# One load for the first pair's K, the third pair's norms on VectorE and its squares on GpSimd, and all instruction orders written anew

## The chip, the cores and the metric

The kernel runs on one core of a Trainium2 chip. A core has five engines that run side by side, each through its own list of instructions in order: TensorE (PE: matrix products and transposes; its weight loads are listed as PEld), VectorE (DVE), ScalarE (ACT), GpSimd (POOL) and SyncE (SP), which only issues transfers here. They meet through semaphores alone: an instruction waits until those it needs have counted up. TensorE writes to PSUM, a small memory of eight banks; everything else lies in SBUF, and 16 DMA engines carry data between it and the device's memory.

The metric is the device time of one execution in microseconds (us). Lower is better.

## The reference

Attention over cosine similarities: 8 batches of 12 heads, 512 rows of 64 numbers each in Q, K and V, in float32.

```python
Q_norm = Q / (np.linalg.norm(Q, axis=-1, keepdims=True) + 1e-10)
K_norm = K / (np.linalg.norm(K, axis=-1, keepdims=True) + 1e-10)
scores = np.einsum('bhqd,bhkd->bhqk', Q_norm, K_norm) / tau        # tau = 0.1
weights = np.exp(scores - np.max(scores, axis=-1, keepdims=True))
weights = weights / (np.sum(weights, axis=-1, keepdims=True) + 1e-10)
return np.einsum('bhqk,bhkd->bhqd', weights, V).astype(np.float32)
```

The scores lie between -10 and 10, so the kernel takes no maximum off before the exponential. The sum of the weights comes out of the second product, since V carries a column of ones.

## The kernel before, in words

The 96 heads are worked through as 48 pairs of heads, pair 0 to pair 47 (the first pair is pair 0, the third is pair 2). Each step of a pair is one entry with a name; the number behind it is the pair.

- LD.s.0 and LD.s.1 load Q and K of pair s (256 KB each, both heads, line 410), LV.s loads V (line 413). 18 buffers hold Q and K, six hold V.
- SQ.s.0 squares Q and K of a pair in one GpSimd instruction of 128x1024 (line 263). For pairs 1 and 2 Q and K are squared apart: SQ.s.0 (Q) on ScalarE (line 261), SQ.s.1 (K) on GpSimd.
- SSQ.s adds the squares of each row in groups with 16 products on TensorE (line 279), and RED.s.0 on VectorE finishes the sum (line 286). For eight pairs, named DIRECT, VectorE alone does it (line 268, RED.s.0 and RED.s.1).
- The reciprocal square root of the sums is made in one of two ways. For pairs 0 to LOGGED - 1 it is a logarithm and an exponential on ScalarE: LN (line 291) and EX (line 295). For the others it is made on VectorE with a bit trick and two Newton steps: NEW.g.0 to NEW.g.7 (lines 381, 372, 373, 377) for a group g of pairs at once. The group sizes stand in GROUPS, whose last number holds for all the rest.
- SCL.s.0 and SCL.s.1 scale Q and K to bf16 (line 302), Q on VectorE, K on VectorE or GpSimd as the table ON says.
- TR.s transposes both on TensorE (line 309), EVA.s copies the result to SBUF on VectorE (line 462). SSQ and TR use one PSUM bank in turn: who comes next in TensorE's list waits until VectorE has read what was there. For seven pairs K's transposes are a transposing DMA, XT.s (line 453).
- SCO.g are the products of K and Q (line 472) and EXP.g the exponentials on ScalarE (lines 497 and 500). From pair 1 on one EXP takes two blocks of 512 scores, so a pair has four of them. Four PSUM banks hold scores, so an SCO waits for the EXP two before it.
- VC.s copies V to bf16 on GpSimd (line 506), PV.s.h.t are the products of weights and V on TensorE (line 520), RCP.s and NRM.s divide by the sum on VectorE (lines 541 and 543), ST.s stores (line 547). Weights are kept for six pairs, so PV runs some pairs behind EXP.

Pair 0 is treated apart, in the function head(), for the sake of an early start: each half (one head) of Q and K goes its own way. Names carry w (0 for Q, 1 for K) and h (the head): LD.0.w.h (line 324; Q from SyncE's queue, K from ScalarE's), SQ.0.w.h, RED.0.w.h, LN.0.w.h, EX.0.w.h, SCL.0.w.h, TR.0.w.h (line 348), EVA.0.w.h (line 319). K of pair 0 is only copied to bf16 (line 320); its norm goes into the scale of the exponentials EXP.0 to EXP.7, each 128x512. Dummy products, warm.k and fill.k (line 248), stand between TensorE's first steps.

Nothing is scheduled while the kernel runs. A list for each engine, the table ORDER, says in which order its entries are issued, and each entry waits for what it needs. So an entry that waits holds up all entries behind it on its engine.

## Time and profile before

| what | us |
|---|---|
| median of three runs | 194.03 (193.59 to 194.36) |
| the profiled execution | 193.27 |
| its span, from the first to the last instruction | 191.5 |
| ScalarE busy in the span | 183.2 (96%) |
| TensorE busy in the span | 179.0 (93%) |
| GpSimd busy in the span | 154.6 (81%) |
| VectorE busy in the span | 152.0 (79%) |
| start of the first exponential, EXP.0 | 7.94 |
| start of the first exponential of pair 1, EXP.8 | 13.78 |

How to read the lines: in the timeline a row has the start in us, the time it took, the engine, the line of the kernel, the operation, what it writes and reads with the shapes, and how many instructions were merged (xN). In square brackets stand the idle time of the engine just ahead and who ended it. In the groups of instructions the numbers behind the bar are the busy time in us and the mean in ns, behind the second bar the idle time ahead of them. Instructions of one engine overlap: the next can start before the last has ended. In the list of issues, the last number is the time from a transfer's issue to its landing.

### The profile page before, as it was taken

Reading aid. Unit: us, or ns where it says so; the run is one execution under the profiler, and the core shown is the slowest. Engines: PE = TensorE matmul, PEld = TensorE weight load, DVE = VectorE, ACT = ScalarE, POOL = GpSimd, SP = SyncE. Lnnn points to the kernel's source line nnn. Section 1 sums busy time; section 2 is a strip of 40 time slices with the busy share of each in tenths; the row PEclk is TensorE's granted clock in tenths of the full one; section 3 lists DMA queues with packets and bytes.
Section 4 is the critical chain, followed back from the end, with each engine's and each line's share of the span. In section 5 each row is a group of like instructions: output and inputs, shape, how many; then the busy total and the mean of one; then the engine's idle time right before and its main releaser. Section 6 shows DMA issues by size and latency. Waiting matters only on the chain.

```text
span 191.5 us, 7081 instructions
## 1 busy us (share of the span) xinstructions
PE 179.0 (93%) x2940; PEld 116.4 (61%) x2940; DVE 152.0 (79%) x454; ACT 183.2 (96%) x217; POOL 154.6 (81%) x143
## 2 busy tenths in 40 slices
...
GB/s 157 340 354 351 348 350 349 350 240 363 365 363 348 267 356 380 377 233 342 322 330 357 264 361 363 365 304 165 234 323 223 82 58 186 125 55 55 113 78 201
DMA packets 56257, 51.72 MB, mean 270 GB/s; under 512 B 6944, under 2 KB 56224, under 8 KB 56224
## 3 DMA queue, kind: packets, MB, share of 16 engines
...
q10 hardware_dynamic: 432, 0.33, 0.5%
q14 instruction: 10, 0.08, 0.1%
HBM read 37.75 MB, written 12.58 MB: 263 GB/s over the span
## 4 chain that ended last, share of the span: by engine, by line
ACT 50%; PE 32%; POOL 9%; DVE 4%; issue 2%; DMA 2%; SPq 0%; POOLq 0%
ACT et L500 50%; PE scps L472 11%; PE ops L520 11%; POOL sq L263 6%; PE xps L309 4%; PE xps L279 3%; DMA qk<-in_Q_dram 2%; POOL qn L302 1%; POOL vb L506 1%; DVE qt L462 1%; DVE qn L302 1%; PE nps L248 1%; DVE ob L576 1%; PE xps L348 0%; PE nps L559 0%
## 5 line engine op out<-in xcount | busy, mean ns | idle before, releaser
L500 ACT ACTIVATE et<-scps 128x1024 bf16<-128x1024 f32 (+1 forms) x190 | 173.4, 1076 | 0.9 <-PE scps L472 0.8
L263 POOL TENSOR_TENSOR sq<-qk 128x1024 bf16<-128x1024 f32 (+2 forms) x49 | 88.2, 1814 | 2.1 <-DMA qk<-in_K_dram 2.1
L472 PE MATMUL scps<-qt 64*128 64x512 bf16 x384 | 75.7, 386 | 5.3 <-ACT et L500 4.0
L520 PEld LDWEIGHTS ops<-vb,et 128*128 128x128 bf16 x1504 | 53.4, 98 | 25.9 <-issue 15.6
L520 PE MATMUL ops<-vb,et 128*128 128x65 bf16 x1504 | 68.3, 194 | 0.3 <-DVE ob L543 0.2
L302 POOL TENSOR_TENSOR qn<-qk,rk 128x512 bf16<-128x512 f32 x36 | 37.3, 1051 | 13.7 <-DVE rk L377 11.2
L302 DVE TENSOR_TENSOR qn<-qk,nps 128x512 bf16<-128x512 f32 x54 | 35.7, 678 | 0.2
L462 DVE COPY qt<-xps 128x1024 bf16<-128x1024 bf16 (+1 forms) x47 | 30.4, 646 | 6.3 <-PE xps L309 6.0
L543 DVE TENSOR_TENSOR ob<-ops,rd 128x512 f32<-128x512 f32 x47 | 32.4, 690 | 1.0
L472 PEld LDWEIGHTS scps<-qt 64*128 64x128 bf16 x384 | 18.9, 92 | 22.1 <-ACT et L500 7.6
L506 POOL TENSOR_SCALAR vb<-vf 128x512 bf16<-128x512 f32 x48 | 29.6, 635 | 1.7 <-DMA vf<-in_V_dram 1.7
L309 PE MATMUL xps<-ident,qn 128*128 128x128 bf16 x348 | 27.4, 220 | 0.8 <-POOL qn L302 0.7
L279 PEld LDWEIGHTS xps<-sq,ident 128*128 128x128 bf16 x624 | 20.7, 97 | 8.6 <-issue 3.7
L279 PE MATMUL xps<-sq,ident 128*128 128x64 bf16 x624 | 25.0, 192 | 0.9 <-POOL sq L263 0.6
L309 PEld LDWEIGHTS xps<-ident,qn 128*128 128x128 bf16 x348 | 19.7, 98 | 9.3 <-DVE rd L541 2.5
L541 DVE RECIPROCAL rd<-ops 128x8 f32<-128x8 f32 x47 | 9.6, 204 | 11.8 <-PE ops L520 11.4
L286 DVE TENSOR_REDUCE nps<-xps 128x16 f32<-128x64 f32 x37 | 8.5, 230 | 7.1 <-PE xps L279 6.8
L268 DVE TENSOR_REDUCE nps<-sq 128x8 f32<-128x512 bf16 x16 | 10.8, 683 | 0.1
L373 DVE SCALAR_TENSOR_TENSOR nps<-nps,ys 128x32 f32<-128x32 f32 (+1 forms) x46 | 9.0, 196 | 1.1
L372 DVE TENSOR_TENSOR nps<-nps,ys 128x32 f32<-128x32 f32 (+1 forms) x46 | 8.9, 194 | 1.0
L497 ACT ACTIVATE et<-scps,xr 128x512 bf16<-128x512 f32 x8 | 5.1, 684 | 0.0
L377 DVE SCALAR_TENSOR_TENSOR nps<-nps,ys 128x16 f32<-128x16 f32 (+1 forms) x28 | 4.7, 175 | 0.3
...
## 6 DMA issues: line engine op xcount, KB each, us to landing
vf<-in_V_dram SPq DMA_DIRECT2D x48, 256.0 KB, 6.1
qk<-in_K_dram SPq DMA_DIRECT2D x47, 256.0 KB, 6.3
qk<-in_Q_dram SPq DMA_DIRECT2D x47, 256.0 KB, 6.2
out_dram<-ob SPq DMA_DIRECT2D x47, 256.0 KB, 5.0
qk<-in_Q_dram SPq DMA_DIRECT2D x2, 128.0 KB, 2.9
qk<-in_K_dram ACTq DMA_DIRECT2D x2, 128.0 KB, 3.1
out_dram<-ob SPq DMA_DIRECT2D x1, 128.0 KB, 2.1
qt<-qn SPq DMA_TRANSPOSE x7, 4.5
```

The lines of the kernel that those rows point to most:

```text
L263: emit = lambda e: e.tensor_tensor(out=b, in0=a, in1=a, op=ALU.mult)
L268: lambda e: e.tensor_reduce(out=dst, in_=sq[s % R_SQ][:, lo:hi, :], axis=AX.X, op=ALU.add))
L279: last = e.matmul(out=x_ps[:, 0:64], lhsT=ident[:, :], rhs=sq[s % R_SQ][:, :, 4 * k : 4 * k + 4], start=(k == 0), stop=(k == 15))
L302: lambda e: e.tensor_tensor(out=qn[iqn][:, w].rearrange("p t h d -> p h t d"), in0=qk[iq][:, w].rearrange("p h (t d) -> p h t d", t=NT), i ...
L309: last = e.transpose(dst[:, i, :], qn[s % R_QN][:, b // NT, b % NT].rearrange("p h d -> p (h d)"), ident[:, :])
L462: lambda e, lo=lo, hi=hi: e.tensor_copy(out=qt_all[:, lo:hi], in_=tb[:, lo:hi]))
L472: last = e.matmul(out=sc_ps[:, (v + i) % BANKS, :], lhsT=qt[p % R_QT][64 * h : 64 * h + 64, 1, c, :], rhs=qt[p % R_QT][64 * h : 64 * h + 6 ...
L500: P.add(("EXP", g2), "act", needs, lambda e, o=o, i=i: e.activation(out=o, in_=i, func=ACT.Exp, scale=inv_tau))
L506: lambda e: e.tensor_scalar(out=vb[:, iq, :, :, 0:DIM].rearrange("p c h d -> p h c d"), in0=vf[iv][:, :, :].rearrange("p h (c d) -> p h c ...
L520: last = e.matmul(out=bank[:, 65 * t : 65 * t + 65], lhsT=e_block(s, c, h, t), rhs=vb[:, iq, c, h, :], start=(c == 0), stop=(c == NT - 1))
L541: lambda e: e.reciprocal(out=rd[io][:, :], in_=grid[:, :, :, DIM]))
L543: lambda e: e.tensor_tensor(out=ob[io][:, :], in0=grid[:, :, :, 0:DIM], in1=rd[io][:, :].unsqueeze(3).to_broadcast([128, 2, NT, DIM]), op= ...
```

## The change

- Pair 0's K is loaded by one transfer of 256 KB, LD.0.1, for both heads, instead of two of 128 KB. Everything that reads K of pair 0 (SQ.0.1.h, SCL.0.1.h) waits for the whole.
- LOGGED goes from 3 to 2 and GROUPS from [1, 2] to [1, 1, 2]: pair 2's norms are made by Newton steps, as a group of its own. LN.2, EX.2.0 and EX.2.1 disappear from ScalarE's list; there are 24 groups of Newton steps, where there were 23.
- ON gets the entry SQ.2.0, which puts the squares of pair 2's Q on GpSimd.
- FILL goes from 17 to 11: six dummy products fewer.
- All five lists of ORDER are new. K of a pair is now mostly loaded ahead of Q, the first loads go more in the order of the pairs (some K loads, of pairs 5, 6, 9 and 12 among them, stand a few places ahead), and on ScalarE LN.0.0.0 and EX.0.0.0 stand ahead of SQ.0.0.1, and LN.0.1.1 and EX.0.1.1 behind EXP.1.

```diff
     def head():
-        for w, h in ((0, 0), (1, 0), (0, 1), (1, 1)):
-            P.add(("LD", 0, w, h), "act" if w else "sp", ["table"] if w else [], lambda e, w=w, h=h: e.dma_start(
-                out=qk[0][:, w, h], in_=src(K if w else Q, 0)[:, h]), slot=f"first{w}{h}")
+        for h in range(2):
+            P.add(("LD", 0, 0, h), "sp", [], lambda e, h=h: e.dma_start(
+                out=qk[0][:, 0, h], in_=src(Q, 0)[:, h]), slot=f"first{h}")
+        P.add(("LD", 0, 1), "act", ["table"], lambda e: e.dma_start(out=qk[0][:, 1], in_=src(K, 0)), slot="first2")
...
             for w in range(2):
-                squares(0, engine("pool", "SQ", 0, w, h), (w, h), 512 * w + 256 * h, 512 * w + 256 * h + 256, [("LD", 0, w, h)])
+                load = ("LD", 0, 1) if w else ("LD", 0, 0, h)
+                squares(0, engine("pool", "SQ", 0, w, h), (w, h), 512 * w + 256 * h, 512 * w + 256 * h + 256, [load])
...
-GROUPS = [1, 2]
-LOGGED = 3
+GROUPS = [1, 1, 2]
+LOGGED = 2
...
-FILL = 17
-ON = {'SQ.0.0.0': 'act', 'SQ.0.1.0': 'pool', ... 'SCL.17.1': 'dve'}
+FILL = 11
+ON = {'SQ.0.0.0': 'act', 'SQ.0.1.0': 'pool', ... 'SCL.17.1': 'dve', 'SQ.2.0': 'pool'}
 ORDER = {
     "sp": """
-        LD.0.0.0 LD.0.0.1 LD.1.1 LD.1.0 LD.2.0 LD.2.1 LD.3.1 LD.3.0 LD.5.0 LD.4.0 LD.5.1 LV.1 LD.4.1 LV.0 LD.7.0
-        LD.6.1 LD.6.0 LV.2 LD.7.1 LD.8.1 LD.9.1 LD.8.0 LD.9.0 LD.13.1 LD.11.0 LD.11.1 LD.13.0 LV.3 LD.14.0
-        LD.10.1 LD.10.0 LV.4 LV.5 LD.12.1 LV.7 LD.14.1 LV.8 LD.12.0 LD.15.1 LV.9 LD.16.1 LD.19.0 LV.6 LD.15.0
+        LD.0.0.0 LD.0.0.1 LD.1.1 LD.1.0 LD.2.1 LD.2.0 LD.5.1 LD.3.1 LD.3.0 LD.4.1 LD.4.0 LD.6.1 LD.5.0 LD.9.1
+        LD.7.0 LD.6.0 LV.0 LD.7.1 LV.1 LD.8.1 LV.3 LD.8.0 LV.2 LD.12.1 LD.9.0 LD.11.0 LD.13.0 LD.10.1 LD.12.0
+        LV.6 LD.11.1 LD.10.0 LV.4 LD.13.1 LV.5 LD.17.0 LD.17.1 LD.20.1 LD.15.1 LD.19.0 LD.16.0 LV.7 LD.15.0
...
     "pool": """
-        one eye SCL.0.1.0 SQ.0.1.0 SQ.0.1.1 SCL.0.1.1 SQ.1.1 vone SQ.2.1 SCL.1.1 SQ.3.0 SQ.5.0 SQ.4.0 VC.0
-        SQ.6.0 SQ.7.0 VC.2 VC.1 SQ.8.0 SQ.9.0 VC.3 SQ.13.0 SQ.10.0 SQ.11.0 SQ.14.0 VC.5 SCL.8.1 SCL.9.1 VC.9
+        one eye vone SQ.0.1.1 SQ.0.1.0 SCL.0.1.0 SCL.0.1.1 SQ.1.1 SQ.2.1 SQ.2.0 SCL.1.1 SQ.3.0 SQ.4.0 SQ.5.0
+        SQ.6.0 VC.0 SQ.7.0 VC.3 SQ.8.0 VC.2 SQ.9.0 VC.1 SQ.12.0 SQ.11.0 SQ.13.0 SQ.10.0 VC.6 SCL.8.1 SCL.9.1
...
-        SCL.19.1 SCL.18.1 SQ.25.0 SQ.26.0 SQ.27.0 SCL.20.1 VC.19 SCL.21.1 VC.21 VC.22 VC.24 SQ.29.0 VC.17
-        SQ.28.0 SCL.22.1 SCL.23.1 VC.26 SQ.30.0 VC.23 SQ.32.0 SQ.31.0 SCL.24.1 VC.25 SCL.25.1 VC.27 VC.29 VC.28
+        SQ.23.0 SCL.18.1 VC.20 SCL.19.1 SQ.27.0 SCL.20.1 SQ.26.0 SCL.21.1 VC.23 VC.21 VC.25 SQ.28.0 VC.24
+        SQ.29.0 SCL.22.1 SCL.23.1 SQ.30.0 SQ.32.0 SQ.31.0 SCL.24.1 VC.22 VC.26 VC.27 SCL.25.1 VC.30 SCL.27.1
...
     "dve": """
-        wz RED.0.0.0 RED.0.0.1 EVA.0.1.0 SCL.0.0.0 RED.0.1.0 RED.0.1.1 EVA.0.0.0 SCL.0.0.1 RED.1.0 EVA.0.0.1
-        EVA.0.1.1 SCL.1.0 RED.2.0 EVA.1 SCL.2.0 SCL.2.1 RED.3.0 NEW.0.0 NEW.0.1 NEW.0.2 NEW.0.3 NEW.0.4 NEW.0.5
-        EVA.2 NEW.0.6 NEW.0.7 SCL.3.0 RED.5.0 SCL.3.1 RED.4.0 NEW.1.0 NEW.1.1 NEW.1.2 NEW.1.3 EVA.3 NEW.1.4
+        wz RED.0.0.0 SCL.0.0.0 RED.0.0.1 RED.0.1.0 EVA.0.0.0 SCL.0.0.1 EVA.0.1.0 EVA.0.0.1 RED.0.1.1 EVA.0.1.1
+        RED.1.0 SCL.1.0 RED.2.0 NEW.0.0 NEW.0.1 NEW.0.2 NEW.0.3 EVA.1 NEW.0.4 NEW.0.5 NEW.0.7 NEW.0.6 SCL.2.1
+        SCL.2.0 RED.3.0 NEW.1.0 NEW.1.1 NEW.1.2 NEW.1.3 EVA.2 NEW.1.4 NEW.1.5 NEW.1.7 NEW.1.6 SCL.3.1 RED.4.0
+        SCL.3.0 RED.5.0 NEW.2.0 NEW.2.1 NEW.2.2 NEW.2.3 EVA.3 NEW.2.4 NEW.2.5 NEW.2.7 NEW.2.6 SCL.4.1 RED.6.0
+        SCL.4.0 RED.7.0 SCL.5.1 NEW.3.0 EVA.4 NEW.3.1 NEW.3.2 SCL.5.0 NEW.3.3 NEW.3.4 NEW.3.5 NEW.3.7 NEW.3.6
...
     "pe": """
-        warm.0 warm.1 warm.2 warm.3 warm.4 warm.5 warm.6 warm.7 warm.8 warm.9 warm.10 fill.0 fill.1 TR.0.1.0
-        warm.11 warm.12 fill.2 fill.3 fill.4 TR.0.0.0 warm.13 warm.14 TR.0.1.1 fill.5 SCO.0 SCO.1 fill.6 SSQ.1
-        fill.7 fill.8 fill.9 fill.10 TR.0.0.1 SCO.2 SCO.3 fill.11 SSQ.2 SCO.4 SCO.5 SCO.6 TR.1 SCO.7 fill.12
-        fill.13 fill.14 fill.15 fill.16 SCO.8 SSQ.3 SCO.9 TR.2 SCO.10 SCO.11 SSQ.5 SCO.12 SSQ.4 SCO.13 TR.3
-        SCO.14 SCO.15 SSQ.6 SCO.16 SSQ.7 PV.0.0.0 SCO.17 PV.0.0.1 SCO.18 TR.4 PV.0.0.2 PV.0.0.3 SCO.19 PV.0.1.0
+        warm.0 warm.1 warm.2 warm.3 warm.4 warm.5 warm.6 warm.7 warm.8 warm.9 warm.10 warm.11 warm.12 fill.0
+        fill.1 fill.2 fill.3 fill.4 TR.0.0.0 warm.13 warm.14 TR.0.1.0 TR.0.1.1 fill.5 TR.0.0.1 SCO.0 SCO.1
+        fill.6 SSQ.1 SCO.2 SCO.3 SCO.4 SCO.5 fill.7 fill.8 fill.9 fill.10 SSQ.2 SCO.6 TR.1 SCO.7 SCO.8 SSQ.3
+        SCO.9 SCO.10 TR.2 SCO.11 SCO.12 SSQ.4 SCO.13 SSQ.5 SCO.14 TR.3 SCO.15 PV.0.0.0 PV.0.0.1 SCO.16 SSQ.6
+        SCO.17 PV.0.0.2 SSQ.7 SCO.18 PV.0.0.3 TR.4 SCO.19 SCO.20 PV.0.1.0 SCO.21 TR.5 SCO.22 PV.0.1.1 SCO.23
+        SSQ.9 SCO.24 TR.6 SCO.25 PV.0.1.2 PV.0.1.3 SCO.26 TR.7 SCO.27 PV.1.0.0 PV.1.0.1 SCO.28 SSQ.8 PV.1.0.2
+        SCO.29 PV.1.0.3 PV.1.1.0 PV.1.1.1 SCO.30 PV.1.1.2 PV.1.1.3 SCO.31 SSQ.10 SCO.32 PV.2.0.0 PV.2.0.1
+        PV.2.0.2 PV.2.0.3 SCO.33 TR.8 PV.2.1.0 SCO.34 PV.2.1.1 PV.2.1.2 PV.2.1.3 SCO.35 TR.9 SCO.36 PV.3.0.0
...
     "act": """
-        table LD.0.1.0 LD.0.1.1 SQ.0.0.0 SQ.0.0.1 LN.0.0.0 EX.0.0.0 LN.0.0.1 EX.0.0.1 LN.0.1.0 EX.0.1.0 LN.0.1.1
-        EX.0.1.1 SQ.1.0 EXP.0 EXP.1 LN.1 SQ.2.0 EX.1.1 EX.1.0 EXP.2 EXP.3 EXP.4 LN.2 EXP.5 EX.2.1 EX.2.0 EXP.6
+        table LD.0.1 SQ.0.0.0 LN.0.0.0 EX.0.0.0 SQ.0.0.1 LN.0.0.1 EX.0.0.1 LN.0.1.0 EX.0.1.0 SQ.1.0 EXP.0 EXP.1
+        LN.1 LN.0.1.1 EX.1.1 EXP.2 EX.1.0 EX.0.1.1 EXP.3 EXP.4 EXP.5 EXP.6 EXP.7 EXP.8 EXP.9 EXP.10 EXP.11
...
```

240 lines of the change are left out of this document (117 added, 123 removed).

## The prediction

> **What bounds the kernel now.** I read the busy shares and the chain of the page first, then ScalarE's groups by shape, its waits and the busy time by stretch, and last the timeline of the first 24 us, where the change has its parts.
>
> ```profile
> PE 179.0 (93%) x2940; PEld 116.4 (61%) x2940; DVE 152.0 (79%) x454; ACT 183.2 (96%) x217; POOL 154.6 (81%) x143
> ...
> ACT 50%; PE 32%; POOL 9%; DVE 4%; issue 2%; DMA 2%; SPq 0%; POOLq 0%
> ```
>
> ```profile
> L500 ACT ACTIVATE et<-scps 128x1024 bf16<-128x1024 f32 x187 | 172.3, 1084 | 0.9 <-PE scps L472 0.8
> ```
>
> ```profile
> 24.00:60.00 36.00, 34.00 (x556) 21.80 (x554) 32.89 (x95) 36.00 (x40) 34.30 (x29) 1.00 1.12 342
> 60.00:100.00 40.00, 38.31 (x646) 25.14 (x646) 32.24 (x104) 39.68 (x44) 40.00 (x37) 1.00 1.06 326
> 100.00:140.00 40.00, 39.61 (x694) 26.45 (x693) 33.92 (x101) 39.95 (x45) 39.52 (x36) 1.00 1.01 299
> ```
>
> In the windows the columns are PE, PEld, DVE, ACT, POOL. ScalarE is the bound: its 187 large exponentials take 172.3 us and it idled 0.9 us ahead of them. Once they run, nothing but ScalarE's own work sets the end. A gain can come only from an earlier start, from work taken off ScalarE, and from those 0.9 us: there is little to win. But the others are close behind: GpSimd has no idle time at all from 60 to 100, TensorE 0.39 us from 100 to 140. An order that makes one of them late costs directly.
>
> ```profile
> 3.23 0.42 ACT L261 ACTIVATE sq<-qk 128x256 bf16<-128x256 f32 x1 [1.14 <-DMA qk<-in_Q_dram]
> ...
> 3.47 0.41 POOL L320 TENSOR_SCALAR qn<-qk 128x256 bf16<-128x256 f32 x1 [2.10 <-DMA qk<-in_K_dram]
> ...
> 4.72 0.42 ACT L261 ACTIVATE sq<-qk 128x256 bf16<-128x256 f32 x1 [1.07 <-DMA qk<-in_Q_dram]
> ...
> 4.94 0.61 POOL L263 TENSOR_TENSOR sq<-qk 128x256 bf16<-128x256 f32 x1 [0.48 <-DMA qk<-in_K_dram]
> ...
> 5.52 0.41 POOL L320 TENSOR_SCALAR qn<-qk 128x256 bf16<-128x256 f32 x1
> ...
> 5.84 0.40 DVE L342 TENSOR_TENSOR qn<-qk,ops 128x256 bf16<-128x256 f32 x1
> ...
> 6.17 0.73 DVE L268 TENSOR_REDUCE xs<-sq 128x4 f32<-128x256 bf16 x2
> ...
> 6.96 0.41 PE L348 MATMUL ops<-ident,qn 128*64 128x128 bf16 x4
> ...
> 7.52 0.60 PE L472 MATMUL scps<-qt 64*128 64x512 bf16 x2
> ...
> 7.94 1.26 ACT L497 ACTIVATE et<-scps,xr 128x512 bf16<-128x512 f32 x2
> ...
> 9.22 0.61 ACT L261 ACTIVATE sq<-qk 128x512 bf16<-128x512 f32 x1
> ...
> 9.74 0.19 ACT L295 ACTIVATE xr<-xl 128x8 f32<-128x8 f32 x1
> ...
> 11.02 5.60 POOL L263 TENSOR_TENSOR sq<-qk 128x1024 bf16<-128x1024 f32 x3
> ...
> 11.77 0.21 ACT L291 ACTIVATE xl<-xs 128x16 f32<-128x16 f32 x1
> 11.87 0.68 ACT L497 ACTIVATE et<-scps,xr 128x512 bf16<-128x512 f32 x1
> ...
> 12.44 0.28 ACT L295 ACTIVATE ops<-xl 128x8 f32<-128x8 f32 x2
> ...
> 12.64 1.26 ACT L497 ACTIVATE et<-scps,xr 128x512 bf16<-128x512 f32 x2
> 12.78 1.28 DVE L302 TENSOR_TENSOR qn<-qk,ops 128x512 bf16<-128x512 f32 x2
> ...
> 13.78 8.36 ACT L500 ACTIVATE et<-scps 128x1024 bf16<-128x1024 f32 x9
> ...
> 22.62 1.94 ACT L500 ACTIVATE et<-scps 128x1024 bf16<-128x1024 f32 x2 [0.49 <-PE scps L472]
> ```
>
> The first exponential (EXP.0) starts at 7.94, the first large one (EXP.8) at 13.78; between them lie 5.84 us. From 13.78 on a large one starts every 0.92 us (nine in 8.36), with one stall of 0.49 ahead of 22.62.
>
> **Part 1, pair 0's K in one load.** Both halves of K now land together, at a time T that the trace doesn't have.
>
> ```profile
> qk<-in_K_dram ACTq DMA_DIRECT2D x2, 128.0 KB, 3.1
> qk<-in_K_dram SPq DMA_DIRECT2D x1, 256.0 KB, 4.3
> ```
>
> ```profile
> 0.84 0.87 ACTq L324 DMA_DIRECT2D qk<-in_K_dram  x2
> ...
> 1.72 0.43 SPq L410 DMA_DIRECT2D qk<-in_K_dram  x1
> ```
>
> The 256 KB row is pair 1's K, issued at 1.72, so landed at 6.0. Lower bound of T: the first half of pair 0's K was there at 3.47, when GpSimd began on it. Upper: a load of the double size issued at 0.84 that takes the 4.3 us of the other, 5.14. The second half was there at 4.94; its bytes are now issued with the first half's, some 0.4 us earlier (half of the 0.87). The same 512 KB of Q and K still share the same engines, so I don't give it all of that, but half: T = 4.7.
>
> What waits for T is more than now. The K copies, SCL.0.1.0 and its transposes TR.0.1.0, ran on the first half from 3.47, ahead of everything; now GpSimd does both squares first and the copies behind them. RED.0.1.0, which waits for GpSimd's second square, stands on VectorE ahead of EVA.0.0.0, SCL.0.0.1 and both other copies of pair 0, and all of these must be through before the first score. What no longer waits is LN.0.0.0: it stood behind SQ.0.0.1 and so behind Q's second half (4.72). Q's first half is now scaled by about 5.0, but it then waits for K. So the head is a trade of one wait for another, and T decides it.
>
> The rest follows the new orders, each operation by its row and the start of the next by the distance in the rows. GpSimd: SQ.0.1.1 at T, SQ.0.1.0 0.58 later, done T+1.2, both K copies done T+1.95. VectorE starts one operation of 256 elements every 0.33: RED.0.1.0 at T+1.22, EVA.0.0.0, SCL.0.0.1 (done T+2.3), EVA.0.1.0 (done T+2.6). TensorE: TR.0.1.1 to T+2.45, a filler, TR.0.0.1 from T+2.6, SCO.0 at T+2.95, and EXP.0 0.42 later as from 7.52 to 7.94: T+3.37. With T = 4.7 that is 8.07, 0.13 later than now. It can't come before 7.65 whatever T is: Q's second half was there at 4.72, its squares (0.42) and sums hold VectorE till 5.5, and RED.0.1.0 stands behind them.
>
> The Trainium skill (DMA: Bandwidth & Descriptors, Anatomy of one DMA) gives a load 2.0 us and its bytes at 436 GB/s, fitted for another issue path; an estimate by it is 2.6 us for 256 KB, T = 3.4. The trace agrees for the lone first halves and not for the 4.3 us row; by the page the sum would be 0.4 us lower, that of EXP.0 at 7.65.
>
> **Part 2, pair 2's squares and norms off ScalarE.** ScalarE loses SQ.2.0 (9.22 to 9.74, 0.52), LN.2 (0.10) and two EX.2 (0.20): 0.82. Against that LN.0.1.1 and EX.0.1.1 now stand behind EXP.1 (0.10 each), and EX.1.1 waits for LN.1, 0.05 to 0.1. By steps: EXP.0 at T+3.37, EXP.1 +3.99, LN.1 +4.65, EXP.2 +5.02, EXP.3 +5.82, then one every 0.6, EXP.8 at T+8.85: 5.48 instead of 5.84. EXP.8 comes at 13.55, 0.23 earlier than now.
>
> GpSimd gains SQ.2.0 as 128x512. SCL.1.1 waited for ScalarE in the gap before it, so the new one falls into that gap:
>
> ```profile
> 8.32 1.04 POOL L263 TENSOR_TENSOR sq<-qk 128x512 bf16<-128x512 f32 x1 [0.49 <-DMA qk<-in_K_dram]
> ...
> 10.01 1.04 POOL L302 TENSOR_TENSOR qn<-qk,xr 128x512 bf16<-128x512 f32 x1 [0.66 <-ACT ops L295]
> ```
>
> SQ.1.1 ends at T+2.96, SQ.2.1 at 4.0, SQ.2.0 at 5.0 (its load must have landed: it is the sixth 256 KB now, and the sixth of before was there at 8.32, when GpSimd began on it), SCL.1.1 at T+6.2 = 10.9; it ends at 11.05 now. EX.1.1, which SCL.1.1 needs, comes at T+4.92, so it is GpSimd's own queue that sets SCL.1.1. The long squares of pair 3 behind it start as before (11.02), and this move costs nothing; without that gap it would cost GpSimd its 1.04.
>
> VectorE gains eight Newton steps for pair 2 alone.
>
> ```profile
> 12.17 0.69 DVE L462 COPY qt<-xps 128x1024 bf16<-128x1024 bf16 x1 [0.92 <-PE xps L309]
> ...
> 14.52 0.18 DVE L372 TENSOR_TENSOR nps<-nps,ys 128x16 f32<-128x16 f32 x1
> ...
> 14.73 0.18 DVE L373 SCALAR_TENSOR_TENSOR nps<-nps,ys 128x16 f32<-128x16 f32 x1
> ...
> 16.06 0.24 DVE L377 SCALAR_TENSOR_TENSOR nps<-nps,ys 128x8 f32<-128x8 f32 x2
> ```
>
> A step is 0.21 (14.52 to 14.73), the last two 0.24 together: 1.55 us, on an engine whose chain now runs without a gap from SCL.1.0 (T+5.8, behind EX.1.0). A new wait comes with it: TensorE sums pair 2's squares ahead of TR.1 in the same bank, so TR.1 waits for RED.2.0, which stands behind SCL.1.0 on VectorE. Copies and scalings of a pair start 0.6 apart. RED.2.0 +6.4, EVA.1 +7.4 (done 8.1), SCL.2.1 +8.75, SCL.2.0 done +10.0, TR.2 to +10.9, EVA.2 done +11.65. SCO.12 then can start at +11.75, its exponential 0.42 later, and EXP.12, due four exponentials after EXP.8 at T+12.53, isn't late: 0.35 us of cover is left. The same working gives EVA.3 done +15.4 against EXP.16 due +16.2 (0.3 left after the score), and for pair 4 RED.7.0 +17.75, EVA.4 done +19.6, EXP.18 and EXP.20 late by about 0.1 in all. So of the present stall of 0.49 some 0.1 stays: -0.39. Where this cover is gone, each 0.1 us that VectorE is late costs 0.1. The six fillers fewer (dummy matmuls) neither cost nor save: they run where TensorE waits.
>
> **Part 3, loads and all orders.** Which loads come when is worked out from the place in SP's list. Pair 1's K, the third 256 KB, landed at 6.0, V of pair 3, the 28th, at 26.2 (19.20 and 7.0): 0.81 us each.
>
> ```profile
> vf<-in_V_dram SPq DMA_DIRECT2D x1, 256.0 KB, 7.0
> ```
>
> ```profile
> 19.20 0.66 SPq L413 DMA_DIRECT2D vf<-in_V_dram  x1
> ...
> 21.40 1.21 POOL L506 TENSOR_SCALAR vb<-vf 128x512 bf16<-128x512 f32 x2
> ...
> 34.88 2.05 POOL L302 TENSOR_TENSOR qn<-qk,rk 128x512 bf16<-128x512 f32 x2
> ```
>
> GpSimd is the engine that this decides: squares every 1.85 (11.02, three in 5.60), V's copies every 0.6. Its new list has SQ.8.0 at 21.4 and SQ.12.0 at 27.1, both waiting for their loads (LD.8.0 is the 22nd, LD.12.0 the 29th), SQ.13.0 at 31.1 (34th), SQ.10.0, VC.6 and then SCL.8.1 at 35.4; now it is at 34.88 with the same number of squares and V copies ahead of it. TR.8 stands ahead of SCO.34, and EXP.34 is due at 37.6; going back over the score, one PV, the transposes and 1.05 us of scaling, SCL.8.1 must start by 35.15. So 0.25 us is lost there. Bounds: nothing, if loads come at the 0.77 between the third (6.0) and the sixth (8.32), which brings LD.13.1 by 29.9; about 2 us, if GpSimd waits for each of three loads as long as it waits in all between 24 and 60 (36.00 less 34.30, 1.7). I take 0.25, the working by the longer row of loads, since the sum of GpSimd's work up to there is the same. SP's stores, V loads and DMA transposes: same number, each a place or two away; I cost them at nothing, covered by V loads several pairs ahead. The end, PV.47 and the last store, follows the last exponential as before.
>
> **The sum**, against the profiled 193.27: EXP.0 +0.13, its way to EXP.8 -0.36, the stall -0.39, SCL.8.1 +0.25: -0.37, 192.9. The median of the plain runs is 194.03; the same difference gives 193.66, rounded 193.6.
>
> **Rivals.**
> 1. Faster, 192.5: K lands by 4.3, so EXP.0 is at 7.65 and EXP.8 at 13.13 (-0.65), GpSimd loses nothing and of the 0.9 us of stalls all go: -1.5. For it: the 2.6 us that the first halves took; against it: the 4.3 us row, and that three engines have to hit every due time.
> 2. Slower, 195.5: GpSimd is late. One place, SCL.8.1 (and SCL.24.1 again, as GpSimd stays full to 100): if it starts after 35.15, TensorE waits at TR.8 with SCO.34 and the PVs behind it, and ScalarE loses the same. With one square's worth of waiting (1.85) more than forecast, 193.66 + 1.85. For it: zero idle time of GpSimd from 60 to 100, and LD.5.1, LD.9.1 and LD.12.1 drawn ahead of loads that are used sooner; against it: one V copy fewer ahead of SCL.24.1 than now.
> 3. VectorE is late: pairs 2 to 4 each miss their due time by 0.3, which adds 0.9: 194.5. Against it: cover of 0.35 and 0.3; for it: no gap in its list from T+5.8 to T+15.
> 4. The one load brings nothing: T = 5.14, EXP.8 0.44 later than forecast at 14.0, 194.1. For it: its one row of the same size; against it: the earlier issue.
>
> **How the numbers follow.** Forecast 0.30, rivals 0.22, 0.30, 0.10, 0.08. What a measurement here can tell from no change is about 0.5%, 1 us: 193.06 to 195.0. Faster is rival 1: 0.22. Slower is rival 2 and a part of 3: 0.34. Same is the rest: 0.44. The forecast's own range is 193.1 to 194.2; to leave out no more than 2 in 10, the range goes from rival 1's 192.5 to 196.4, one and a half squares (2.8) above the forecast, as the wait of rival 2 can come more than once.
>
> **What would show it.** In the trace after: one K load on ScalarE's queue landing near 4.7, EXP.0 near 8.1, EXP.8 near 13.5; two groups of Newton steps of 128x16 on VectorE instead of one, with EVA.2 done near 16.4; SCL.8.1 starting near 35.4; ScalarE's idle time ahead of the large exponentials about 0.7, the most of it near 37. I am wrong if that idle time is above 2 us (then rival 2 or 3, by whether GpSimd or VectorE has no gap before it), or if EXP.8 is before 13.2.

## The result and the profile after

The changed kernel took 191.82 us (median of six, 191.37 to 192.19); the kernel before, measured beside it, 194.19 (median of six, 193.59 to 195.51). The ratio is 0.986, 95% interval 0.982 to 0.990: faster by 1.4%, some 2.4 us. The prediction, 193.6 with a range of 192.5 to 196.4 and its largest chance (0.44) on "same", was wrong.

The profiled executions stand badly for the two kernels. That of before took 193.27, at the low end of what this kernel does (192.8 to 196.8 in all comparisons below), that of after 192.19, the slowest of its six. So the two traces differ by 1.1 us where the medians differ by 2.4, and what follows leans on several traces of each kind.

The page of the changed kernel: busy time of the engines, and the shares of the chain that ended last.

```profile
PE 178.2 (94%) x2934; PEld 115.9 (61%) x2934; DVE 155.3 (82%) x462; ACT 182.5 (96%) x213; POOL 155.7 (82%) x144
...
ACT 43%; POOL 31%; PE 9%; DVE 7%; issue 4%; DMA 3%; SPq 1%; POOLq 0%
```

ScalarE is as busy as before. The shares of busy time say nothing of 2.4 us; the chain now runs through GpSimd for 31%, where it ran through TensorE.

The timeline of the changed kernel's head, rows of all engines.

```profile
0.82 0.45 ACTq L326 DMA_DIRECT2D qk<-in_K_dram  x1
...
4.01 1.18 POOL L263 TENSOR_TENSOR sq<-qk 128x256 bf16<-128x256 f32 x2 [1.85 <-DMA qk<-in_K_dram]
...
6.72 0.63 ACT L261 ACTIVATE sq<-qk 128x512 bf16<-128x512 f32 x1 [0.60 <-DMA qk<-in_Q_dram]
6.89 0.60 PE L474 MATMUL scps<-qt 64*128 64x512 bf16 x2
...
7.31 1.27 ACT L499 ACTIVATE et<-scps,xr 128x512 bf16<-128x512 f32 x2
...
15.30 0.68 DVE L464 COPY qt<-xps 128x1024 bf16<-128x1024 bf16 x1
```

The whole K of pair 0 has landed at 3.93, and GpSimd starts on it at 4.01. EXP.0 follows at 7.31, where it was 7.94, and the copy EVA.2 is done at 15.98.

ScalarE's own timeline, first of after, then of before, from the first large exponential to the last. A row runs until the engine is seen idle.

```profile
13.04 22.46 ACT L502 ACTIVATE et<-scps 128x1024 bf16<-128x1024 f32 x24 [0.17 <-PE scps L474]
36.01 88.38 ACT L502 ACTIVATE et<-scps 128x1024 bf16<-128x1024 f32 x96 [0.50 <-PE scps L474]
124.60 62.57 ACT L502 ACTIVATE et<-scps 128x1024 bf16<-128x1024 f32 x70 [0.21 <-PE scps L474]
188.40 0.36 ACTq L582 DMA_DIRECT2D out_dram<-ob  x1
```

```profile
22.62 75.53 ACT L500 ACTIVATE et<-scps 128x1024 bf16<-128x1024 f32 x82 [0.49 <-PE scps L472]
98.43 89.63 ACT L500 ACTIVATE et<-scps 128x1024 bf16<-128x1024 f32 x99 [0.27 <-PE scps L472]
189.29 0.35 ACTq L580 DMA_DIRECT2D out_dram<-ob  x1
```

EXP.8 starts at 13.04 instead of 13.78, 0.74 earlier. The last exponential ends at 124.60 + 62.57 = 187.17 instead of 98.43 + 89.63 = 188.06, 0.89 earlier. From there to the end of the span are 3.29 us instead of 3.48. The idle time ScalarE shows ahead of large exponentials has not gone down: 0.88 in three places after (0.17 ahead of EXP.8 itself, then 0.50 and 0.21), 0.76 in two before. It has moved.

That idle time isn't all the delay, though. In each trace the starts of two large exponentials that nothing holds lie 0.904 us apart (the median of all distances). One takes 1.08 us (before) to 1.19 (a_twok below) by its record, so the records overlap, and an exponential that starts up to 0.2 us late leaves no gap. Two rows from windows of the timeline, of after and of before, with no idle time in either:

```profile
23.49 12.02 ACT L502 ACTIVATE et<-scps 128x1024 bf16<-128x1024 f32 x13
```

```profile
59.10 37.22 ACT L500 ACTIVATE et<-scps 128x1024 bf16<-128x1024 f32 x40
```

Less the last one's own time (1.1), the first is 0.91 per start, the second 0.926: forty exponentials without a gap that lost 0.85 us. I therefore take as delay, for each distance between consecutive starts from EXP.8 on, what it has over 0.905, and add that up by stretch. The kernel before shows 0.76 us of idle time and 3.9 us of delay, the changed one 0.88 and 3.65.

So the 1.1 us between these two traces are 0.74 at the start of EXP.8, 0.25 of delay and 0.19 behind the last exponential, less 0.09 by which the last record is longer. The other 1.3 us of the 2.4 lie between the traces and the medians.

### The profile page after: what moved, and what is told of

Its sections match the earlier page's. It is cut to its first block, busy times and chain, and to the rows that moved or that the text cites. A ratio compares the mean times of both kernels' runs of the same rounds, so it can differ in the third digit from the quotient of the medians.

```text
span 190.5 us, 7076 instructions
## 1 busy us (share of the span) xinstructions
PE 178.2 (94%) x2934; PEld 115.9 (61%) x2934; DVE 155.3 (82%) x462; ACT 182.5 (96%) x213; POOL 155.7 (82%) x144
## 4 chain that ended last, share of the span: by engine, by line
ACT 43%; POOL 31%; PE 9%; DVE 7%; issue 4%; DMA 3%; SPq 1%; POOLq 0%
ACT et L502 43%; POOL sq L263 19%; POOL vb L508 7%; POOL qn L302 5%; PE scps L474 3%; DMA qk<-in_K_dram 3%; PE ops L522 3%; PE xps L279 3%; DVE qn L302 2%; DVE qt L464 1%; PE xps L309 1%; DVE nps L286 1%; DVE nps L375 1%; DVE nps L374 1%; DVE ob L578 1%
## 5 line engine op out<-in xcount | busy, mean ns | idle before, releaser
L263 POOL TENSOR_TENSOR sq<-qk 128x1024 bf16<-128x1024 f32 (+2 forms) x50 | 89.1, 1797 | 6.2 <-DMA qk<-in_K_dram 4.0
L522 PEld LDWEIGHTS ops<-vb,et 128*128 128x128 bf16 x1504 | 52.2, 98 | 23.9 <-issue 15.2
L522 PE MATMUL ops<-vb,et 128*128 128x65 bf16 x1504 | 65.3, 194 | 0.0
L302 POOL TENSOR_TENSOR qn<-qk,rk 128x512 bf16<-128x512 f32 x36 | 37.3, 1048 | 11.6 <-DVE rk L379 11.1
L302 DVE TENSOR_TENSOR qn<-qk,nps 128x512 bf16<-128x512 f32 x56 | 37.1, 680 | 0.2
L383 DVE TENSOR_SCALAR ys<-nps 128x32 int32<-128x32 int32 (+1 forms) x24 | 4.5, 186 | 0.6
```

Of the source, the lines that this page charges most:

```text
L263: emit = lambda e: e.tensor_tensor(out=b, in0=a, in1=a, op=ALU.mult)
L302: lambda e: e.tensor_tensor(out=qn[iqn][:, w].rearrange("p t h d -> p h t d"), in0=qk[iq][:, w].rearrange("p h (t d) -> p h t d", t=NT), i ...
L522: last = e.matmul(out=bank[:, 65 * t : 65 * t + 65], lhsT=e_block(s, c, h, t), rhs=vb[:, iq, c, h, :], start=(c == 0), stop=(c == NT - 1))
```

## The experiments

The question was what carries the gain: the head (part 1), the work taken off ScalarE (part 2), single waits, or the orders as a whole (part 3), and if the orders, through what: GpSimd's work, the loads, or the order on the other engines. Ratios are to the kernel before on the same chip in the same comparison. The theories in an expectation are those of the time when it was written.

| run | median us (range) | ratio, 95% interval | EXP.8 | last EXP ends | from there to the end |
|---|---|---|---|---|---|
| before, first profile | 194.19 (193.59 to 195.51) | | 13.78 | 188.06 | 3.48 |
| b_again | 193.90 (193.21 to 195.44) | 0.9995 [0.9964, 1.0026] | 13.40 | 188.05 | 4.01 |
| b_onek | 193.81 (192.36 to 196.13) | 0.9975 [0.9940, 1.0009] | 13.26 | 188.02 | 3.44 |
| b_vc14 | 193.51 (193.06 to 194.92) | 0.9985 [0.9955, 1.0015] | 13.62 | 187.81 | 3.81 |
| b_lv14 | 193.77 (193.11 to 195.43) | 0.9990 [0.9964, 1.0017] | 13.83 | 188.32 | 4.01 |
| b_vchalf | 193.86 (192.81 to 196.50) | 0.9993 [0.9963, 1.0023] | 13.08 | 189.64 | 4.21 |
| b_lvhalf | 194.02 (192.75 to 194.76) | 0.9979 [0.9947, 1.0011] | 13.91 | 188.69 | 3.97 |
| b_ld7 | 194.10 (193.33 to 195.11) | 1.0014 [0.9987, 1.0040] | 14.04 | 188.12 | 3.88 |
| b_ld7st | 193.46 (192.85 to 194.32) | 0.9982 [0.9955, 1.0009] | 13.65 | 187.95 | 3.28 |
| after | 191.82 (191.37 to 192.19) | 0.9862 [0.9821, 0.9903] | 13.04 | 187.17 | 3.29 |
| a_again | 191.41 (191.01 to 192.37) | 0.9865 [0.9824, 0.9906] | 12.70 | 187.25 | 3.29 |
| a_twok | 191.78 (191.26 to 193.25) | 0.9892 [0.9852, 0.9932] | 13.37 | 186.47 | 3.29 |
| a_logs3 | 192.10 (191.89 to 192.61) | 0.9902 [0.9867, 0.9937] | 13.49 | 186.56 | 3.60 |
| a_sq10 | 191.74 (190.98 to 192.25) | 0.9897 [0.9870, 0.9923] | 12.72 | 185.95 | 3.30 |
| a_vchalf | 191.33 (191.04 to 191.56) | 0.9854 [0.9822, 0.9886] | 12.48 | 186.13 | 3.29 |
| a_lvhalf | 191.76 (191.50 to 193.34) | 0.9890 [0.9852, 0.9927] | 13.26 | 186.50 | 3.30 |

The last three columns come from one trace each. A name with b_ is the kernel before with an edit (b_again: with none), one with a_ the changed kernel with an edit.

### The head: one load alone, and two loads in the changed kernel

```diff
# b_onek: before + the changed kernel's load; a_twok: the reverse edit in the changed kernel
-        table LD.0.1.0 LD.0.1.1 SQ.0.0.0 SQ.0.0.1 LN.0.0.0 EX.0.0.0
+        table LD.0.1 SQ.0.0.0 SQ.0.0.1 LN.0.0.0 EX.0.0.0
```

> The kernel before, unchanged, a second time, to see how far its own executions differ. Theory A (the change gains at the head and in a few stalls that every execution has): ratio 1.000, between 0.997 and 1.003, and a profile like the first: EXP.0 near 7.9, EXP.8 near 13.8, ScalarE idle ahead of the large exponentials 0.9 us. Rival B (the old orders lose 1 to 2 us in many executions, which the one profile of before didn't show): the profile has more than 1.5 us of such idle time, in one or two places, or the single times spread over more than 1 us.

> The kernel before with one load for pair 0's K and nothing else changed; GpSimd still copies the first half before it squares it. Theory A: all of K is there near 4.0 instead of 3.5 and 4.9, but Q's second half, which LN.0.0.0 stands behind, also lands some 0.3 us earlier; EXP.0 near 7.6, EXP.8 near 13.45, 0.3 to 0.4 us less than before, ratio 0.998. Rival B (the orders carry the gain): ratio 1.000 and the same stalls as before.

> The changed kernel with pair 0's K in two loads of 128 KB again, all orders as changed. Theory A: GpSimd's first square waits for the second half (4.7 to 4.9), EXP.0 comes 3.37 later at 8.1 to 8.3 instead of 7.31, and the end moves by 0.8 to 1.0 us: 192.7, ratio 0.992 to 0.993. Rival B: the later start is lost again in waits for loads and GpSimd that are there anyway, 191.8 to 192.1.

ScalarE's timeline of b_onek, and what TensorE waited for ahead of the first stall:

```profile
13.26 36.08 ACT L502 ACTIVATE et<-scps 128x1024 bf16<-128x1024 f32 x39
50.07 74.58 ACT L502 ACTIVATE et<-scps 128x1024 bf16<-128x1024 f32 x81 [0.73 <-PE scps L474]
125.22 62.80 ACT L502 ACTIVATE et<-scps 128x1024 bf16<-128x1024 f32 x70 [0.56 <-PE scps L474]
```

```profile
49.10 0.61 PE L309 MATMUL xps<-ident,qn 128*128 128x128 bf16 x8 [0.65 <-POOL qn L302]
```

The stall at 22.6 is gone, but the time comes back at 50, where TensorE waits for GpSimd's scaling, and at 125: the last exponential ends at 188.02. The kernel before, run again, also started 0.38 earlier than in its first profile and ended its last exponential at the same 188.05. In the changed kernel two loads cost a later start, and this trace runs on in one piece:

```profile
13.37 173.10 ACT L500 ACTIVATE et<-scps 128x1024 bf16<-128x1024 f32 x190
```

It ends at 186.47, before either trace of the unedited changed kernel, which started earlier. The medians can't tell a gain of some 0.5 us from none here: the load alone has 0.9975 with an interval that holds 1, and the interval of 0.9892 without it overlaps those of 0.9862 and 0.9865 with it. Undoing the head leaves a gain of 1.1%: the head isn't what carries most of it.

### Part 2 undone

```diff
-GROUPS = [1, 1, 2]
-LOGGED = 2
+GROUPS = [1, 2]
+LOGGED = 3
# SQ.2.0, LN.2, EX.2.1, EX.2.0 back on ScalarE's list, NEW.0 off VectorE's
```

> The changed kernel with pair 2's norms by logarithm and exponential on ScalarE again and its Q squares on ScalarE; the other orders as changed (the entries taken out of VectorE's and GpSimd's lists, put back into ScalarE's where they stood). Theory A: 0.52 + 0.10 + 0.20 us of work come back onto ScalarE between EXP.1 and EXP.6, some of it in a wait that is there anyway: 0.5 to 0.8 us longer, 192.3 to 192.6, ratio 0.990 to 0.992. Rival (the gain is in the orders, ScalarE catches up): 191.8 to 192.0.

192.10, ratio 0.990: with ScalarE's work back, 1.0% of gain is left. Part 2 is worth 0.3 us by the medians and 0.8 by the ratios (0.9902 against 0.9862 and 0.9865), not told from nothing by the intervals. Its EXP.8 is 0.45 to 0.8 later than in the changed kernel's traces, and as in a_twok the last exponential ends no later (186.56).

### Single waits

```diff
# b_vc14, GpSimd's list of before: VC.14, which waited for its load, four places later
-SCL.14.1 VC.14 SCL.15.1 VC.18 VC.13 VC.11 VC.16
+SCL.14.1 SCL.15.1 VC.18 VC.13 VC.11 VC.14 VC.16
# b_lv14, SyncE's list of before: that load earlier
-ST.2 LD.24.0 LD.23.0 LD.24.1 LD.25.1 LD.23.1 LV.14 ST.3
+ST.2 LV.14 LD.24.0 LD.23.0 LD.24.1 LD.25.1 LD.23.1 ST.3
# a_sq10, GpSimd's list of after: the square that TensorE waits for at 35.0 one place earlier
-SQ.12.0 SQ.11.0 SQ.13.0 SQ.10.0 VC.6
+SQ.12.0 SQ.11.0 SQ.10.0 SQ.13.0 VC.6
```

> The kernel before with one entry moved on GpSimd: VC.14, which waits 1.70 us for its V load at 58.7 in both profiles of before, stands three V copies and one scaling later. Theory G (GpSimd is never idle from 20 to 145 in the old orders, so what it loses it can't make up, and it sets the end): the 1.7 us come back, the stalls behind 58 disappear, ratio 0.992 to 0.997, and the spread of the times gets smaller. Rival S (ScalarE alone sets the end, GpSimd's wait is covered): ratio 0.999 to 1.001.

> The kernel before with one entry moved on SyncE: V's load of pair 14 is issued five loads earlier; GpSimd's list as before. Theory G: the same gain from the other side, GpSimd's wait at 58.7 shrinks to under 0.3 us, ratio 0.992 to 0.997. Rival S: 0.999 to 1.001. If the five Q and K loads that are now one place later are what GpSimd waits for next, the wait moves there and nothing is won.

> The changed kernel with the squares of pairs 13 and 10 in the other order on GpSimd, as TensorE's sums of pair 10 stand ahead of SCO.32 and waited 0.88 us for them at 35.0. If that stall of 0.5 us is in every execution: 191.3 to 191.5, ratio to before 0.985 to 0.987, 0.3 to 0.5 us under the changed kernel. If it is given back later (GpSimd sets the pace on the way): no difference from the changed kernel's 191.8.

The first two take away a wait of GpSimd that stands in the profile of before, in a stretch where it is otherwise full; the row of before:

```profile
58.75 0.63 POOL L506 TENSOR_SCALAR vb<-vf 128x512 bf16<-128x512 f32 x1 [1.70 <-DMA vf<-in_V_dram]
```

In b_vc14 the wait is gone and GpSimd has no gap from 24 to 60, but the trace has stalls of ScalarE of 0.78 at 22.75 and 0.30 at 125.02; b_lv14 has 0.51 at 50.40 and 0.61 at 125.53, and GpSimd waits 0.71 for another V load at 45.80. Neither is faster (0.9985 and 0.9990, both intervals hold 1). In the changed kernel the wait behind the stall at 36.01 is this one, TensorE's row:

```profile
35.00 0.65 PE L279 MATMUL xps<-sq,ident 128*128 128x64 bf16 x16 [0.88 <-POOL sq L263]
```

a_sq10 has no stall at 36 and the earliest end of the last exponential in the table, 185.95, but the median is 191.74: no difference from the changed kernel either. One wait taken away is not a gain in any of the three.

### More work for GpSimd

```diff
-'SCL.10.1': 'dve', 'SCL.11.1': 'dve'
+# both on GpSimd, in its list behind VC.4
```

> The changed kernel with two more scalings on GpSimd (K of pairs 10 and 11, 2.1 us) instead of VectorE. Theory G: the changed orders have their gain from GpSimd being ahead; it then has too little left, TensorE waits for it near 74 and 97, and 0.5 to 2 us are lost: 192.3 to 193.8. Rival S: 191.8, as VectorE is freer and GpSimd ends at 155 in any case.

197.47 (196.67 to 199.14), ratio 1.019 [1.016, 1.023], beyond both theories. Two scalings of 1.05 us cost 5.7 us, far more than their work, and by a wait. The waits of this run, longest in total first, in us, times and the longest:

```profile
POOL qn L302 <- DVE rk L379: 15.6, 8, 5.1
...
ACT et L502 <- PE scps L474: 5.9, 3, 4.7
```

The unedited changed kernel has 11.1 us in 5 waits, the longest 5.1 as well, in the first of these rows, so 4.5 us in three waits are new. The place that costs, in GpSimd's and then in TensorE's rows:

```profile
40.12 2.04 POOL L302 TENSOR_TENSOR qn<-qk,rk 128x512 bf16<-128x512 f32 x2 [2.56 <-DVE rk L379]
...
50.14 0.63 POOL L508 TENSOR_SCALAR vb<-vf 128x512 bf16<-128x512 f32 x1
```

```profile
50.82 0.84 PE L522 MATMUL ops<-vb,et 128*128 128x65 bf16 x12 [4.57 <-POOL vb L508]
51.59 0.61 PE L474 MATMUL scps<-qt 64*128 64x512 bf16 x2
```

GpSimd waits 2.56 us for VectorE's factors ahead of the two moved scalings and holds up the squares and V copies behind them: the copy at 50.14 was at 46.11 in the changed kernel, and TensorE waits 4.57 us for it. TensorE's clock falls with it. Its granted clock is 0.50 from 48.8 to 55.6, and two products of a score take 0.61 us there instead of 0.39, and ScalarE waits twice more (0.48 and 0.73). An entry in the wrong place costs what is queued behind it.

### Orders crossed

```diff
# h_dvepe: before's VectorE and TensorE lists with after's SyncE, GpSimd and ScalarE lists (one K load, LOGGED = 3, FILL = 11)
# b_front: before, its first 120 SyncE and 90 GpSimd entries in the order that they have after
-LD.3.1 LD.3.0 LD.5.0 LD.4.0 LD.5.1 LV.1 LD.4.1 LV.0
+LD.5.1 LD.3.1 LD.3.0 LD.4.1 LD.4.0 LD.6.1 LD.5.0 LD.9.1
...
# a_front: after, the same parts in the order that they had before
# a_again: after, unchanged
```

> A hybrid: loads' and GpSimd's lists of the changed kernel, VectorE's and TensorE's lists of before, pair 2's norms on ScalarE as in a_logs3 (192.1) and one K load. Theory G (the new order of the loads and of GpSimd carries the gain): 191.8 to 192.6, ratio 0.988 to 0.992. Rival P (TensorE's and VectorE's new lists carry it): 193.5 to 194.3, ratio 0.997 to 1.001. Third possibility, each set of lists only fits its own: above 194.5.

> The kernel before with the first 120 entries of SyncE's list and the first 90 of GpSimd's (to about 97 us) in the new lists' relative order, behind pair 0 to 2; all else as before. Theory G: most of the gain but what the head and the rest of GpSimd's list bring, 192.0 to 192.8, ratio 0.989 to 0.994. Rival P: no change, 193.8 to 194.3. If lists only fit their own: above 194.5.

> The counterpart: the changed kernel with the same parts of SyncE's and GpSimd's lists in the old relative order. Theory G: the gain is lost, 193.3 to 194.3, GpSimd without idle time till 145 and stalls near 98 and 125. Rival P: 191.8 to 192.2. If lists only fit their own: above 194.5.

> The changed kernel once more, beside the hybrids: 191.4 to 192.2, ratio 0.985 to 0.989; EXP.0 within 0.4 us of 7.3 and EXP.8 within 0.4 of 13.0. If the end of the last exponential follows the start of EXP.8 from profile to profile, the head counts; if it doesn't, it is set later.

Medians 218.10 (ratio 1.122 [1.116, 1.128]), 210.88 (1.085 [1.080, 1.091]) and 213.46 (1.097 [1.092, 1.102]): each mixture costs 17 to 24 us against the kernel that it was made from, in both directions. ScalarE's wait for scores in h_dvepe, in b_front and in a_front:

```profile
ACT et L502 <- PE scps L474: 18.3, 15, 3.1
```

```profile
ACT et L500 <- PE scps L472: 15.4, 16, 2.8
```

```profile
ACT et L502 <- PE scps L474: 21.4, 19, 7.6
```

The lists are fitted to each other. The size of the cost is not theirs alone, though. In these three traces TensorE's granted clock is 0.50 for 13.7, 13.7 and 20.5 us, in stretches of 3.4 us (one of 10.2), each at a wait of TensorE of 1.6 us or more. If TensorE did half its work there, the clock made 7 to 10 us of the cost, an estimate and an upper bound, since TensorE also waits inside these stretches. Of the traces in the table above, b_vchalf's alone has such a stretch ahead of the end. So no single list could be shown to carry the gain this way, and an exchange of one whole list between the kernels wasn't tried on the chip.

### Lighter GpSimd, lighter loads

```diff
# b_vchalf, a_vchalf: V copies of pairs 18 to 47 for the first head alone
-out=vb[:, iq, :, :, 0:DIM]...  in0=vf[iv][:, :, :]...
+out=vb[:, iq, :, 0 : 2 if s < 18 else 1, 0:DIM]...  in0=vf[iv][:, 0 : 2 if s < 18 else 1, :]...
# b_lvhalf, a_lvhalf: V loads of pairs 18 to 47 for the first head alone
-e.dma_start(out=vf[iv][:, :, :], in_=src(V, s))
+e.dma_start(out=vf[iv][:, 0:n, :], in_=src(V, s)[:, 0:n, :])      # n = 2 if s < 18 else 1
```

> Left out of the computation: for pairs 18 to 47 the V copy on GpSimd (line 507) copies the first head only, so the second head's values are those of an older pair. Each of these 30 copies goes from 0.63 us to about 0.33, 9 us less work for GpSimd between 58 and 141 us; nothing else is touched. Theory G (in the old orders GpSimd, which has no idle time from 60 to 100, sets the end): 191.5 to 192.5, a gain of about 2, with GpSimd idle for some us before 145 and its executions closer together than the 3 us of the kernel before. Theory L (the loads set it): 194.0, since the same bytes come at the same times. Theory S (the order on VectorE and TensorE, or ScalarE itself): 193.7 to 194.3.

> The same part left out (second head of the V copy of pairs 18 to 47) of the changed kernel. Theory G: at most 0.3 below the changed kernel (191.5 to 191.9), since its orders leave GpSimd 4 us of idle time between 120 and 145 already. Theory S, with GpSimd a cost in both: as large a step as in the kernel before, whichever that is.

> Left out of the computation: for pairs 18 to 47 only the first head of V is loaded (128 KB less in each of 30 loads), so the second head's values are those of an older pair; GpSimd's copies keep their size. Theory L (late loads set the end in the old orders): 192.0 to 192.8, and GpSimd's waits for V and K loads at 58 and 119 us are gone. Theory G: 193.5 to 194.2, since GpSimd has as much to do and only its waits for loads, some 2.2 us, may go; if these count in full, 192.5. Theory S: 194.0.

> The same part left out (second head of the V loads of pairs 18 to 47) of the changed kernel. Theory G: 191.4 to 191.9, no change. Theory L: at most 0.5 lower, by the 1.35 us that GpSimd waits for a V load at 129 us.

My theory was that the old orders are slow because GpSimd has no slack from 58 to 145. Busy time by stretch, in columns PE, PEld, DVE, ACT, POOL, of before and of b_vchalf:

```profile
58.00:100.00 42.00, 40.15 (x680) 26.28 (x678) 34.14 (x108) 41.68 (x46) 41.25 (x38) 1.00 1.06 328
100.00:145.00 45.00, 44.61 (x792) 30.00 (x791) 38.20 (x112) 44.91 (x50) 44.52 (x41) 1.00 1.02 305
```

```profile
58.00:100.00 42.00, 40.66 (x687) 26.61 (x686) 34.32 (x107) 42.00 (x47) 39.45 (x39) 1.00 1.03 325
100.00:145.00 45.00, 43.39 (x773) 29.12 (x770) 37.58 (x109) 44.15 (x49) 39.94 (x39) 1.00 1.02 299
```

b_vchalf gives GpSimd 7.6 us of idle time in these 87 us, where it had 1.2, and is no faster: 193.86, ratio 0.9993. With half of the V bytes gone from pair 18 on (b_lvhalf) it is 194.02. The changed kernel doesn't move either (191.33 and 191.76). Both theories fall: after 58 us neither GpSimd's amount of work nor the V loads set the time of either kernel.

### Early loads and last stores

What was left is where the delay sits. The table has the mean over nine traces of the kernel before and its variants with the old orders, and over seven of the changed kernel and its variants (those of the table above), from the starts as described.

| us | old orders | new orders | difference |
|---|---|---|---|
| start of EXP.8 | 13.62 | 13.01 | 0.61 |
| delay to 24 us | 0.85 | 0.48 | 0.37 |
| delay, 24 to 60 | 0.61 | 0.49 | 0.12 |
| delay, 60 to 100 | 1.04 | 0.62 | 0.42 |
| delay, 100 to 140 | 1.10 | 1.07 | 0.03 |
| delay from 140 on | 0.73 | 0.41 | 0.32 |
| last EXP to the end (b_ld7st left out) | 3.85 | 3.34 | 0.51 |

The differences add up to 2.4 us; the medians of the same kernels differ by 2.1 on average (193.9 and 191.7). Part of the rest is one trace: b_vchalf's execution took 195.59 us, 1.7 over its median, with the granted clock at half for 3.4 us from 21.3 on. Without it the sum is 2.2, with 0.7 for the start and 0.2 for the first stretch. The two traces of the unedited changed kernel don't stand for its median either: both are the slowest of their six, with 3.65 and 4.1 us of delay against 2.6 to 3.2 in its variants. And the table says where the time lies, not what caused it, since an earlier start can be given back further on. No part has a third of the whole. Two rows are steady: from 140 us on every old trace has 0.71 to 0.75 and every new one 0.40 to 0.44; and the end after the last exponential is 3.4 to 4.2 us in the old and 3.3 in all new ones but one (3.6).

The delay from 140 on can be followed to its place. In all nine old traces the same five exponentials are late, EXP.146, 157, 171, 189 and 192, by 0.59 to 0.63 us together; in all seven new ones it is EXP.167, 184 and 185 instead, by 0.28 to 0.30. No edit of loads, copies, squares or stores changed that. TensorE's rows ahead of EXP.146, which starts at 141.99, in the kernel before:

```profile
140.30 0.39 PE L472 MATMUL scps<-qt 64*128 64x512 bf16 x2
140.62 0.64 PE L279 MATMUL xps<-sq,ident 128*128 128x64 bf16 x16
141.10 0.53 PE L520 MATMUL ops<-vb,et 128*128 128x65 bf16 x12
141.56 0.39 PE L472 MATMUL scps<-qt 64*128 64x512 bf16 x2
```

TensorE is never idle here: its list has the sums SSQ.38 and three products with V between SCO.145 and SCO.146, and the second score comes 1.26 us behind the first, where one exponential takes 0.904. So this 0.3 us of the change is read from the traces as TensorE's new order; no run moved these entries alone. From 60 to 100 it looks alike: at least 0.54 us of the delay falls on the same six exponentials in every old trace, about 0.1 on the same two in every new one.

For the first stretch and for the end I made an edit each:

```diff
# b_ld7 and b_ld7st: pair 4's and pair 7's K load ahead of V of pairs 1 and 2
-LD.5.1 LV.1 LD.4.1 LV.0 LD.7.0 LD.6.1 LD.6.0 LV.2 LD.7.1 LD.8.1
+LD.5.1 LD.4.1 LV.0 LD.7.0 LD.6.1 LD.6.0 LD.7.1 LV.1 LV.2 LD.8.1
# b_ld7st alone: the last stores in order of pairs
-XT.45 ST.41 ST.43 ST.40 ST.45 ST.42 ST.44 ST.46
+XT.45 ST.41 ST.40 ST.42 ST.43 ST.44 ST.45 ST.46
```

> The kernel before with three entries of SyncE's list moved: both K loads of pairs 4 and 7 come ahead of the V loads of pairs 1 and 2, so pair 7's K load is issued two loads earlier (loads of 256 KB land 0.75 us apart, so it lands near 18.0 instead of 19.5). Theory E (in the old orders late loads in the first 24 us, and GpSimd behind them, set when TensorE can go on): GpSimd's wait at 19.5 (0.48 in the profile of before) and ScalarE's stall at 22.6 (0.49) go, the start of EXP.24 comes 0.4 to 0.7 earlier, and the time falls to 193.4 to 193.8. Theory G (GpSimd's own work sets it): the stall moves to 50 us or stays, the time is 193.9 to 194.2.

> The same with the last stores on SyncE's list in order of pairs (ST.42, ST.44 no longer behind ST.45, ST.40 no longer behind ST.43). Theory F (in the old orders three 256 KB stores issued together at 184.7 to 186.0 us hold up the last four, which land 3.4 to 4.0 us after ScalarE's last exponential; 3.3 in the changed kernel): they are issued by 181 apart from ST.45, the end of the span comes 3.3 us after the last exponential, 0.2 to 0.7 less than in the kernel with the loads alone, and the time is that much lower (193.0 to 193.4 if theory E holds as well). If the last stores' time is their own, nothing changes.

b_ld7 does what it was made for and gains nothing (194.10, ratio 1.001): its first 120 large exponentials run without a gap, where before stalled at 22.6, and then it stalls at 125. ScalarE's timeline:

```profile
14.04 110.82 ACT L500 ACTIVATE et<-scps 128x1024 bf16<-128x1024 f32 x120
125.32 62.80 ACT L500 ACTIVATE et<-scps 128x1024 bf16<-128x1024 f32 x70 [0.45 <-PE scps L472]
```

The stores are another matter. SyncE's stores between 184.0 and 187.3, of before and of b_ld7st, and the landing of the last store (64 KB, us from issue) of before, of b_ld7 and of b_ld7st:

```profile
184.71 1.63 SPq L547 DMA_DIRECT2D out_dram<-ob  x3
```

```profile
184.60 3.06 SPq L547 DMA_DIRECT2D out_dram<-ob  x2
```

```profile
out_dram<-ob ACTq DMA_DIRECT2D x1, 64.0 KB, 1.8
```

```profile
out_dram<-ob ACTq DMA_DIRECT2D x1, 64.0 KB, 2.2
```

```profile
out_dram<-ob ACTq DMA_DIRECT2D x1, 64.0 KB, 1.6
```

In the old list ST.42 and ST.44 stand behind ST.45, which waits until 184.7. Then three stores of 256 KB go out at once, the next at 187.4, and the last ones share the DMA engines with them. In order of pairs, ST.45 goes alone at 184.6 and ST.46 at 187.3. The end comes 3.28 us after the last exponential, 0.60 less than in b_ld7, and the median is 0.64 lower than b_ld7's on the same chip (193.46 against 194.10). That is the end of the changed kernel, 3.29, got by moving three entries of one list. A lone store is slow there too (3.5 us from its issue at 184.6 in b_ld7st), so the landing of the three says little by itself; the last store's says it, as its 1.8, 2.2 and 1.6 us differ by what the ends differ (3.48, 3.88 and 3.28). The two intervals against the kernel before overlap, but the twelve executions of b_ld7 and of b_ld7st, set against each other, differ by 0.66 us in the mean, with a 95% interval of 0.2 to 1.1. Most of the change's gain of 2.4 us is still missing.

## Why the prediction was wrong

- **T, the landing of K.** Forecast 4.7, between bounds of 3.47 and 5.14; measured 3.93. The 256 KB took 3.1 us from their issue, not the 4.3 of the row that I leaned on. The estimate by the Trainium skill (DMA: Bandwidth & Descriptors, Anatomy of one DMA), 2.6 us, was nearer by its T of 3.4 than mine, and 0.5 us too low. Here the mechanism was right and the size off.
- **EXP.0 = T + 3.37.** Measured 7.31 - 3.93 = 3.38. The floor of 7.65 "whatever T is" was wrong, since Q's second half landed earlier too (4.28 instead of 4.70 in the traces).
- **EXP.0 to EXP.8** 5.73, forecast 5.48; EXP.8 at 13.04, forecast 13.55, past the 13.2 that I had named as a mark of being wrong. EVA.2 came at T + 12.05 (15.98), forecast T + 11.65. Of the 0.7 us by which the two traces differ more than I forecast (1.08 against 0.37), 0.5 is this earlier EXP.8.
- **"Once they run, nothing but ScalarE's own work sets the end."** This is the step that failed, together with "those 0.9 us: there is little to win". I read the idle column as all that could be won from late scores. The distances of the starts in the same trace hold 3.9 us. The sign was in my own reading "every 0.92 us": I took it for ScalarE's pace, but where nothing holds them the starts are 0.904 apart, and the 0.016 us between, taken 187 times, are 3 us, hidden in the 172.3 us that I called ScalarE's work. In the means of the traces the delay falls from 4.3 to 3.1 us. And an earlier start was to pay in full: b_again and b_onek start 0.4 and 0.5 earlier than the first profile of before and end their last exponential at the same 188.0; a_twok starts 0.3 to 0.7 later than the changed kernel and ends earlier. In one trace a gain at the head is given back on the way.
- **The stall of 0.49 at 22.6** went, as forecast, and another of 0.50 stands at 36.0. It is near the place where I had put 0.25 ("near 37"), and SCL.8.1 started at 35.50, forecast 35.4. But TensorE waited there for the square SQ.10.0, ahead of SCL.8.1, and a_sq10, which takes this wait away, changes no median. And the 0.1 us that I left for EXP.18 and EXP.20 came as 0.34 at EXP.18 and EXP.19 (0.25 and 0.09 late, without a gap, in each of the seven traces). The sum of shown stalls did not fall, so the -0.39 and the +0.25 are both void as terms.
- **Part 3, "SP's stores ... I cost them at nothing", and "the end, PV.47 and the last store, follows the last exponential as before".** Wrong by 0.5 us in the mean of the traces: b_ld7st shows the place in the list.
- **The rivals.** Rival 1 (192.5) had the right side and the early landing, but its gain of the 0.9 us of stalls did not come; what came instead was spread over the whole run. Rivals 2 and 3 (GpSimd or VectorE late) fell. That the danger of rival 2 is real a_pool2 shows, at 5.7 us.
- **Profile against median.** I carried a difference worked out against 193.27 over to the median. The kernel before varies by 3 us between executions, the changed one by 1.4, and the profile of before lay near the lower end. What the median of before has over that execution, 0.9 us, could not be in a sum made on it. The clock is a part of that spread but not of the gain: of 103 executions of the kernel before beside the experiments, the 18 with a mean granted clock under 0.995 have a median of 194.9 and the other 85 of 194.0, and one of 41 of the changed kernel and its variants in the table is under 0.995.

What the runs leave open: the order of the last stores is shown to be worth about 0.5 of the 2.4 us. The head has 0 to 0.6 us and part 2 has 0.3 to 0.8 by their medians and ratios, neither told from nothing. Of the rest, 0.3 from 140 on goes with TensorE's order by the traces, and some 0.4 between 60 and 100 us sits on fixed exponentials in the same way; no run moves those entries alone. What makes the others is not settled: single repairs of the old orders (a load, a copy, GpSimd's work, V's bytes) only move the delay in their traces, and mixtures of old and new lists are slower than both. No version of these beats the changed kernel by more than the intervals.
